# A hybrid decoder layer: sixth product, row loads and ScalarE order moved, first-half gate multiplies from GpSimd to VectorE

## The chip, the cores and the metric

The kernel runs on one core of one Trainium2 chip. The metric is device time in microseconds (us) of one execution, as the median of three. A core has a matrix engine (TensorE, PE in the profile, with its weight loads shown as PEld), three engines for element work (VectorE = DVE, ScalarE = ACT, GpSimd = POOL) and an engine that here only issues DMAs (SyncE = SP). Each engine takes its instructions in the order in which they were written, and waits for the others by semaphores.

## The reference

The layer normalises its input, projects it once, sends the columns through two mixers, gates both and projects back. Cut to what matters:

```python
xn = rms_norm(x, ln_g)                                    # x: 2048 x 1024
b, c, xc, gc, xl, gl = split(xn @ w_in)                   # w_in: 1024 x 6144
y_conv = b * causal_conv3(c * xc)
y_conv = headwise_rms_norm(y_conv, 8, conv_out_g) * silu(gc)
u = causal_conv4(xl) + lru_conv_b                         # 16 heads of 64
r, i = sigmoid(u @ w_a + b_a), sigmoid(u @ w_i + b_i)     # block-diagonal
log_a = 8 * r * log_sigmoid(lam)
h = scan(exp(log_a), sqrt(-expm1(2 * log_a)) * (i * u))   # h_t = a_t h_(t-1) + drive_t
y_lru = headwise_rms_norm(h, 16, lru_out_g) * silu(gl)
out = rms_norm(x + concat(y_conv, y_lru) @ w_out, final_g)
```

All of it is float32. The two silus (a sigmoid and a multiply) are the "gates" of the title.

## The kernel before

**Products.** A float32 product is made of three matmuls on rounded pieces: each operand is split into a high and a low part (`th`, `tl` for the moving side T, the two halves of a tile `s` for the stationary side S), and `mm` (L1014) issues high-high, high-low and low-high. One product over four blocks `j` is so 12 matmuls of 128x128 by 128x512. Four output quarters are made of seven such products (numbers 0 to 6) instead of eight by sums and differences of the operands' quarters; `s_plan` makes S's sums, `TPrep`, `bit` and the class `Change` make T's.

**Steps.** The program is 64 steps. Steps 0 to 23 are the first half of the positions: for each of 8 blocks `k` one step `l` (recurrent unit, `lru`), `a` (`conv_a`, c and x of the convolution) and `b` (`conv_b`, b and its gate). Steps 24 to 47 do the same for the second half, steps 48 to 63 (`outp`) the output projection in two phases. Steps 0 to 2 are written out with eight products (`plain`, of eight slots of 12 matmuls, with the side work in `after1` and `after2`). Then a step has slots for products 0, 6 (that of the step before, put off), 1, 3, 2, 4, 5. T is changed at steps 24, 48 and 56: such a step has eight plain products, the next one (called late) six in the order 0, 4, 5, 1, 3, 2, and meanwhile `Change.slot` casts the new T. Its `sixth` subtracts and casts the T of product 6, which the step after the late one (26, 50, 58) uses first.

**Order.** All five engines run in written order (`manual_schedule`). `at(n, f)` puts `f` off by n slots, `tick` runs what is due at a slot's start, and `prep(n, s)` makes piece s of a step's S. `defer(f)` holds `f` back while `held` is a list, and `release` runs it. A product's result lies in a PSUM bank; products 0, 1 and 2 of a step add up in one bank, and ScalarE copies what stands there between them (`q`, `u`, `rr`, L1315 to L1321), so TensorE has to wait with the next product of that bank until the copy is done. `put` takes a finished quarter to the mixer. There, `silu` multiplies gate and sigmoid (`gl<-gl,sg`, `gb<-gb,sg`), on GpSimd except in step 24; `gates` issues four small matmuls into two banks of their own, which `sigs` frees with four sigmoids (`r`, `i`, L758); and `m1` (L832) and `mj` (L835) are the width-3 convolution. In `outp`, `load` brings the rows `xr` (the residual) that are added to the result `ob`.

**Bits.** The T pieces of products 1 and 2 for the first half are 16 small jobs (`bits`: subtractions `traw<-traw`, casts `th` at L1160, low parts `tl`), done two to a slot by `do_bits` from the first slot of step 1 on.

## Time and profile before

| | us |
|---|---|
| three runs | 1316.51, 1317.4, 1314.1 |
| median | 1316.51 |
| the profiled execution | 1314.92 |
| its span, first to last instruction | 1313.1 |
| busy: TensorE | 1289.5 (98%) |
| busy: VectorE | 1046.0 (80%) |
| busy: ScalarE | 748.7 (57%) |
| busy: GpSimd | 250.0 (19%) |

The profile is of one execution. Its span is 1.8 us shorter than that execution's own time, and that time is 1.6 us under the median. Rows of the timeline show the start in us from the span's start, the duration in us, engine, line, operation, output and inputs, shapes, and in brackets the idle time of the engine before it with what ended the idle time. `SPq` rows are DMA issues. Rows of the windows view show for each engine its busy us and how many of its instructions fall in the stretch, then the granted TensorE clock (1.00 is full speed), the DMA engines' share and GB/s.

### The profile page before, as it was taken

What the parts mean: (1) busy time and instruction counts of PE and PEld (TensorE: products, weight loads), DVE (VectorE), ACT (ScalarE), POOL (GpSimd) and SP (SyncE); (2) the same over time, 40 slices, a digit from 0 to 9 for tenths busy, and PEclk for the clock granted to TensorE, in tenths of its full rate; (3) what the DMA queues carried; (4) which work ended last, traced back from release to release, by engine and by line L of the source; (5) the groups of instructions that cost most, each with busy time, mean ns of one, the idle gap of its engine ahead of it and who ended that gap; (6) DMA issues with size and microseconds to landing.
All of it is one profiled execution on the core that took longest, in us unless ns stands there. A gap on an engine that the chain in (4) does not pass through costs nothing.

```text
span 1313.1 us, 16711 instructions
## 1 busy us (share of the span) xinstructions
PE 1289.5 (98%) x5688; PEld 1061.0 (81%) x5688; DVE 1046.0 (80%) x1284; ACT 748.7 (57%) x1141; POOL 250.0 (19%) x189
## 2 busy tenths in 40 slices
PE   7989999999999999999999999999999999999997
PEld 6867888888888888778888888888888888887886
DVE  6789898999999998967666666667559767649886
ACT  7576767576675667566454645454466433445443
POOL 3204243344435441001010110101011000000000
PEclk9989999999999999999999999999999999999999
DMA  7128887898989887651899999999789986697654
GB/s 294 32 90 290 290 286 264 302 350 283 345 302 329 295 301 280 207 199 33 277 318 296 340 352 333 324 355 362 236 271 339 260 261 229 249 402 273 235 179 160
DMA packets 157958, 355.29 MB, mean 271 GB/s; under 512 B 16944, under 2 KB 51760, under 8 KB 157872
## 3 DMA queue, kind: packets, MB, share of 16 engines
q1 hardware_dynamic: 153264, 338.17, 74.4%
q0 software_dynamic: 4320, 15.73, 3.1%
q8 instruction: 45, 0.74, 0.2%
q14 instruction: 41, 0.34, 0.1%
q10 hardware_dynamic: 288, 0.32, 0.1%
HBM read 217.11 MB, written 137.04 MB: 270 GB/s over the span
## 4 chain that ended last, share of the span: by engine, by line
PE 82%; DVE 8%; DMA 5%; ACT 3%; issue 2%; SPq 0%; POOL 0%; ACTq 0%; DVEq 0%
PE bank L1014 79%; DMA s<-so 2%; DVE tl L163 2%; PE gate L751 2%; DVE traw L163 1%; DMA tl<-td 1%; DMA zr<-rsd 1%; DMA xr<-od 1%; DMA fg<-in_final_g_dram 1%; DVE u L723 1%; ACT i L758 0%; DVE s L163 0%; ACT r L758 0%; ACT th L451 0%; PE tp L554 0%
## 5 line engine op out<-in xcount | busy, mean ns | idle before, releaser
L1014 PE MATMUL bank<-th,s 128*128 128x512 f32 x3632 | 1129.6, 390 | 5.7 <-ACT rr L1318 1.6
L1014 PEld LDWEIGHTS bank<-th,s 128*128 128x128 f32 x3632 | 682.7, 188 | 151.7 <-ACT rr L1318 2.5
L1014 PE MATMUL bank<-tl,s 128*128 128x512 f32 x1816 | 708.2, 390 | 1.8 <-DVE tl L163 1.6
L1014 PEld LDWEIGHTS bank<-tl,s 128*128 128x128 f32 x1816 | 341.4, 188 | 74.5 <-DVE tl L163 3.0
L163 POOL TENSOR_TENSOR s<-raw,s 128x512 fp32r<-128x512 f32 x62 | 115.1, 1870 | 231.1 <-ACT s L213 176.0
L213 ACT CAST s<-raw 128x512 fp32r<-128x512 f32 x140 | 85.4, 618 | 48.4 <-PE bank L1014 32.8
L163 POOL TENSOR_TENSOR gb<-gb,sg 128x1024 f32<-128x1024 f32 x16 | 43.4, 2712 | 335.5 <-ACT sg L682 335.5
L163 DVE TENSOR_TENSOR s<-raw,s 128x512 fp32r<-128x512 f32 (+1 forms) x125 | 91.6, 755 | 10.6 <-ACT s L1073 6.7
L163 DVE TENSOR_TENSOR s<-s,s 128x512 fp32r<-128x512 f32 x105 | 86.6, 824 | 2.1 <-ACT s L213 1.5
L163 DVE TENSOR_TENSOR tl<-traw,th 128x512 fp32r<-128x512 f32 x85 | 60.8, 748 | 19.4 <-ACT th L451 13.4
L213 ACT CAST s<-s 128x512 fp32r<-128x512 f32 x105 | 64.7, 616 | 4.3 <-DVE s L163 4.0
L723 DVE SCALAR_TENSOR_TENSOR u<-xl,pt,u 128x1024 f32<-128x1024 f32 x48 | 61.3, 1278 | 6.1 <-ACT u L719 5.5
L835 DVE SCALAR_TENSOR_TENSOR t<-p,pt,t 128x1024 f32<-128x1024 f32 x32 | 46.5, 1454 | 16.6 <-ACT t L832 15.8
L1315 ACT COPY q<-bank 128x512 f32<-128x512 f32 x58 | 33.9, 584 | 40.9 <-PE bank L1014 31.5
L163 DVE TENSOR_TENSOR st<-u,st 64x512 fp32r<-64x512 f32 x64 | 53.8, 841 | 2.0
L758 ACT ACTIVATE r<-gate,pt 64x512 f32<-64x512 f32 x64 | 43.7, 683 | 17.3 <-PE gate L751 16.5
L1318 ACT COPY rr<-bank 128x512 f32<-128x512 f32 x31 | 18.1, 584 | 53.6 <-PE bank L1014 53.3
L1318 ACT COPY u<-bank 128x512 f32<-128x512 f32 x27 | 15.8, 585 | 52.4 <-PE bank L1014 52.4
L163 DVE TENSOR_TENSOR traw<-traw 128x512 f32<-128x512 f32 x60 | 41.8, 701 | 4.7 <-DMA traw<-in_w_out_dram 3.6
L451 ACT CAST th<-traw 128x512 fp32r<-128x512 f32 x64 | 36.1, 618 | 16.1 <-DVE traw L163 14.2
L758 ACT ACTIVATE i<-gate,pt 64x512 f32<-64x512 f32 x64 | 43.8, 684 | 1.1
L1321 ACT COPY u<-bank 128x512 f32<-128x512 f32 x31 | 18.1, 585 | 43.6 <-PE bank L1014 43.5
(169 smaller groups left out, 1294.1 us busy)
## 6 DMA issues: line engine op xcount, KB each, us to landing
sd<-s SPq DMA_DIRECT2D x151, 512.0 KB
s<-sd SPq DMA_DIRECT2D x151, 512.0 KB
raw<-in_w_in_dram SPq DMA_DIRECT2D x104, 256.0 KB
raw<-yd SPq DMA_DIRECT2D x64, 256.0 KB
traw<-in_w_out_dram SPq DMA_DIRECT2D x64, 256.0 KB
so<-so SPq DMA_DIRECT2D x22, 512.0 KB
s<-so SPq DMA_DIRECT2D x22, 512.0 KB
yd<-gl SPq DMA_DIRECT2D x32, 256.0 KB
```

Source lines behind the costliest of these rows:

```text
L163: (eng or nc.vector).tensor_tensor(out=out, in0=a, in1=b, op=op)
L213: nc.scalar.copy(dst[i][0], val(i))
L451: nc.scalar.copy(self.dst[i, j][0], self.r[i, j])
L723: nc.vector.scalar_tensor_tensor(out=v["u"], in0=o1[:, 1 + j:1 + j + N2], scalar=lw[j], in1=v["u"], op0=ALU.mult, op1=ALU.add)
L751: nc.tensor.matmul(ps[j], v["gw"][n][:, j, :], v["st"][j][:, sl], start=(n == 0), stop=(n == 1))
L758: nc.scalar.activation(out=g_[hi, sl], in_=v["ps"][j][src], func=AF.Sigmoid, bias=pt[src, bias + k:bias + k + 1])
L835: nc.vector.scalar_tensor_tensor(out=tcur["t"], in0=p[:, 2 + j:2 + j + N2], scalar=cw[j], in1=tcur["t"], op0=ALU.mult, op1=ALU.add)
L1014: nc.tensor.matmul(bank, a[:, js], b, start=start and n == 0, stop=stop and n == 2, skip_group_check=more)
L1315: nc.scalar.copy(q1, bk["A"])
L1318: nc.scalar.copy(u2, bk["A"])
L1321: nc.scalar.copy(rr, bk["A"])
```

## The change

The change moves instructions and removes none but for the engine of 16 multiplies. In its parts:

1. First half (`h == 0`): the 16 multiplies of gates and sigmoids in `lru` and `conv_b`, each 128x1024, go from GpSimd to VectorE.
2. Bits: two to a slot in the first six slots of step 1 and then one to a slot in step 2, instead of two to a slot in all of step 1.
3. `hi(5)`, the cast of a step's S piece 5, is deferred behind the ScalarE copy `q`; in late steps of the output, casts of T and S go behind `rr` and `u`.
4. Step 26: product order 0, 3, 6, 1, 2, 4, 5. `sixth` subtracts all four blocks in the late step and casts all four one slot later. `m1` is deferred behind the copy `u`.
5. Step 56: `load` two to three slots sooner (ticks 2 and 3, not 5 and 6).

```diff
@@ s_plan
-                lambda: hi(5),
+                lambda: defer(lambda: hi(5)),
@@ class Change
-        def sixth(self, *js):
-            for j in js:
+        def sixth(self):
+            for j in range(NB):
                 tt(self.r[6, j], self.r[6, j], self.r[1, j], ALU.subtract)
-            self.cut([(6, j) for j in js])
+            at(1, lambda: self.cut([(6, j) for j in range(NB)]))
...
             if q == 21:
-                self.sixth(0, 1)
-                at(1, lambda: self.sixth(2, 3))
+                self.sixth()
@@ lru, put
-                silu(g, late, nc.vector if h and late else None)
+                silu(g, late, nc.vector if late or not h else None)
@@ conv_a, put
-                at(1, m1)
+                at(1, lambda: defer(m1))
@@ conv_b, put
-                silu(g)
+                silu(g, 0, None if h else nc.vector)
@@ outp
-            at(5, lambda: load(0))
-            at(6, lambda: load(1))
+            sooner = 3 if ph == 1 and m == 2 else 0
+            at(5 - sooner, lambda: load(0))
+            at(6 - sooner, lambda: load(1))
@@ after1
-            do_bits(2)
+            if s < 6:
+                do_bits(2)
@@ after2
-            do_bits(2)
+            do_bits(1)
@@ main loop
+            if kind != "o" and n > 1 and opens(n - 2):
+                slots = (0, 3, 6, 1, 2, 4, 5)
...
+                if i == 1 and slots[2] == 6:
+                    held[0] = []
                 tick()
...
                 if late:
-                    change.slot(16 + s)
+                    if i != 1 or kind != "o":
+                        change.slot(16 + s)
...
                 elif s == 0:
+                    held[0] = []
                     prep(n, 6)
...
                 elif s > 0:
-                    held[0] = [] if i == 2 else None
-                    prep(n + 1, s - 1)
+                    if i == 2 and not late:
+                        held[0] = []
+                    if i != 2 or kind != "o" or not late:
+                        prep(n + 1, s - 1)
...
-                if s == 1 and not late:
+                if i == 6 and not late and s < 3:
...
                 if i == 0:
                     q1 = sm_q1[0] = sm("q1")
                     nc.scalar.copy(q1, bk["A"])
+                    release()
                 elif i == 1:
                     u2 = sm_u2[0] = sm(("u2", "rr")[n % 2])
                     nc.scalar.copy(u2, bk["A"])
+                    release()
+                    if late and kind == "o":
+                        change.slot(16 + s)
...
                     if late:
                         put(12, bk["D"], rr)
+                        if kind == "o":
+                            prep(n + 1, s - 1)
```

How the order moves is seen at three places. The first is ScalarE in step 1 and at the start of step 2, from the copy of the bank that holds quarter 22 to the convolution `t<-p`. `th<-traw` is a bit's cast, `r` and `i` are the sigmoids that free the gate banks. Before:

```order
L814 COPY xx<-bank 128x512
L814 COPY p<-bank 128x512
L1160 CAST th<-traw 128x512
L1073 CAST s<-raw 128x512
L1160 CAST th<-traw 128x512
L814 COPY xx<-bank 128x512
L758 ACTIVATE r<-gate,pt 64x512
L758 ACTIVATE i<-gate,pt 64x512
```

and with the change:

```order
L813 COPY xx<-bank 128x512
L813 COPY p<-bank 128x512
L1073 CAST s<-raw 128x512
L813 COPY xx<-bank 128x512
L757 ACTIVATE r<-gate,pt 64x512
L757 ACTIVATE i<-gate,pt 64x512
```

The two casts of bits now stand behind these sigmoids, one after `t<-p`, one after the second set of sigmoids.

The second place is ScalarE in steps 25 and 26 (the change of T between the halves), first from the cast of the recurrent unit's `u` on. Before:

```order
L734 CAST st<-u 64x1024 x2
L451 CAST th<-traw 128x512 x2
L1321 COPY u_5065<-bank 128x512
L451 CAST th<-traw 128x512 x2
L1315 COPY q_5099<-bank 128x512
```

and with the change:

```order
L733 CAST st<-u 64x1024 x2
L1334 COPY u_5059<-bank 128x512
L451 CAST th<-traw 128x512 x4
L1324 COPY q_5099<-bank 128x512
L757 ACTIVATE r<-gate,pt 64x512
```

The bank's copy `u` has moved ahead of the casts for the sixth product. A few rows on, from the last sigmoid of the first set, there stood before:

```order
L758 ACTIVATE i<-gate,pt 64x512
L620 CAST rt<-sums 128x512
L832 ACTIVATE t<-p,pt 128x1024
L1318 COPY u_5149<-bank 128x512
L758 ACTIVATE r<-gate,pt 64x512
L758 ACTIVATE i<-gate,pt 64x512
```

and with the change:

```order
L757 ACTIVATE i<-gate,pt 64x512
L619 CAST rt<-sums 128x512
L757 ACTIVATE r<-gate,pt 64x512
L757 ACTIVATE i<-gate,pt 64x512
L757 ACTIVATE r<-gate,pt 64x512
L757 ACTIVATE i<-gate,pt 64x512
L1328 COPY u_5180<-bank 128x512
L831 ACTIVATE t<-p,pt 128x1024
```

The convolution `t<-p` has moved behind the second set of sigmoids and behind the next copy.

The third place is SyncE's issues in step 56, `xr` being the residual rows, `tl<-td` T's pieces, `s<-so` S's pieces, `raw` and `zr` the inputs of a later step's S. Before:

```order
L518 DMA tl<-td_133 128x512
L239 DMA s<-so_125 128x1024
L894 DMA xr<-od_138 128x1024
L239 DMA s<-so_125 128x1024
L307 DMA raw<-yd_86 128x512 x2
L297 DMA zr<-rsd_89 128x1024
L307 DMA raw<-yd_86 128x512 x2
L297 DMA zr<-rsd_89 128x1024
L894 DMA xr<-od_139 128x1024
```

and with the change:

```order
L239 DMA s<-so_125 128x1024
L893 DMA xr<-od_138 128x1024
L517 DMA tl<-td_130 128x512
L517 DMA tl<-td_131 128x512
L517 DMA tl<-td_132 128x512
L517 DMA tl<-td_133 128x512
L893 DMA xr<-od_139 128x1024
L239 DMA s<-so_125 128x1024 x2
L307 DMA raw<-yd_86 128x512 x2
```

The first row load has moved ahead of four T pieces and one S piece, the second ahead of two S pieces, four `raw` and two `zr`.

## The prediction

> **What bounds the kernel.** I read the page first: busy times, then the chain that ended last.

> ```profile
> PE 1289.5 (98%) x5688; PEld 1061.0 (81%) x5688; DVE 1046.0 (80%) x1284; ACT 748.7 (57%) x1141; POOL 250.0 (19%) x189
> ...
> PE 82%; DVE 8%; DMA 5%; ACT 3%; issue 2%; SPq 0%; POOL 0%; ACTq 0%; DVEq 0%
> ```

> TensorE works in 98% of the span and carries 82% of the chain. The change takes no matmul away, so it can only win what TensorE loses in waits or at a lower clock: 1313.1 - 1289.5 = 23.6 us of idle time, part of it at the start and the end, where nothing is changed. The second view is that of the waits, for TensorE alone (us in total, times, longest):

> ```profile
> PE gate L751 <- ACT i L758: 3.6, 2, 3.4
> ...
> PE bank L1014 <- ACT rr L1318: 1.6, 2, 1.3
> ...
> PE bank L1014 <- DVE xx L163: 1.3, 1, 1.3
> PE bank L1014 <- DVE ob L163: 1.1, 1, 1.1
> PE norm_ps L627 <- ACT i L758: 0.8, 1, 0.8
> ```

> These are few and short. Only seven waits matter, and each lies at a place that the change touches. The third view is TensorE's timeline there. For the longest wait, with two rows of the windows view behind it:

> ```profile
> 69.61 0.40 PE L1014 MATMUL bank<-tl,s 128*128 128x512 f32 x1
> ...
> 73.25 0.39 PE L1014 MATMUL bank<-th,s 128*128 128x512 f32 x1
> 77.05 0.79 PE L751 MATMUL gate<-st,bh 128*128 128x512 f32 x1 [3.41 <-ACT i L758]
> ...
> 84.46 0.39 PE L1014 MATMUL bank<-tl,s 128*128 128x512 f32 x1
> ```

> ```profile
> 76.00:80.00 4.00, 2.77 (x6) 1.76 (x7) 1.99 (x4) 3.92 (x7) 0.00 (x0) 0.62 0.02 4
> 80.00:84.00 4.00, 4.00 (x12) 3.09 (x11) 3.93 (x5) 3.81 (x7) 0.10 (x1) 0.53 0.00 0
> ```

> From 69.61 to 73.25 sixteen matmuls start, so one takes (73.25 - 69.61) / 16 = 0.2275 us at full clock. From 73.25 to 84.46 only 18 start (one, 4 of the gates, 13 of products) in 11.21 us, where 18 x 0.2275 = 4.1 would do. **The place costs 7.1 us**, twice what the list of waits says: 77.05 - 73.25 - 0.23 = 3.57 is the wait, and 3.55 is the clock after it, 0.62 and 0.53 of full speed in the two windows.

> **Place A, steps 1 and 2 (6.6 us).** The gate matmul waits for sigmoids that free its bank. ScalarE's queue ahead of them:

> ```profile
> 73.17 0.62 ACT L1160 CAST th<-traw 128x512 fp32r<-128x512 f32 x1 [2.02 <-DVE traw L163]
> ...
> 74.62 0.62 ACT L1160 CAST th<-traw 128x512 fp32r<-128x512 f32 x1 [0.31 <-DVE traw L163]
> 75.15 0.58 ACT L814 COPY xx<-bank 128x512 f32<-128x512 f32 x1
> 75.62 0.68 ACT L758 ACTIVATE r<-gate,pt 64x512 f32<-64x512 f32 x1
> ```

> Two casts of bits stand there, both idle until VectorE has made their input. The change puts both behind the sigmoids: 2.02 + 0.31 of waiting and 2 x 0.53 of casting go, and the first sigmoid starts at 75.62 - 3.4 = 72.2. VectorE is ahead of this point by another 0.6, worked out below. First sigmoid then at 71.6, first bank free two sigmoids (1.4) later at 73.0, second at 74.4. TensorE is there at 73.25 + 0.23 = 73.5 and needs the second bank at 73.9. It loses about 0.5 instead of 7.1. The casts, moved, come due where products 1 and 2 of step 3 need them, seven slots of 12 x 0.2275 us later at least.

> The trace shows that a 3.4 us wait is followed by a slower clock; the wait of 1.32 quoted for place B is not (granted clock 1.00 over that stretch). Between the two nothing is measured. If 2 us of waiting were left, the place would still cost 2.0 with the clock kept and 2.0 + 3.55 = 5.6 with it lost: gains of 5.1 or 1.5. I keep 1.5 to 7.1 as the ends and take 6.6. [...]

> **VectorE instead of GpSimd (0 us by itself).** Rows for what a multiply costs and what it frees:

> ```profile
> 57.89 2.41 POOL L163 TENSOR_TENSOR gl<-gl,sg 128x1024 f32<-128x1024 f32 x1 [2.89 <-ACT sg L682]
> ...
> 403.38 2.88 POOL L163 TENSOR_TENSOR gb<-gb,sg 128x1024 f32<-128x1024 f32 x1 [3.05 <-ACT sg L682]
> ```

> ```profile
> 58.35 2.50 DVE L163 TENSOR_TENSOR s<-raw,s 128x512 fp32r<-128x512 f32 x1 [2.27 <-ACT s L1073]
> ...
> 403.92 2.89 DVE L163 TENSOR_TENSOR raw<-raw 128x512 f32<-128x512 f32 x1
> ...
> 551.02 1.22 DVE L163 TENSOR_TENSOR gl<-gl,sg 128x1024 f32<-128x1024 f32 x1
> ```

> ```profile
> 318.00:377.00 59.00, 59.00 (x262) 48.77 (x261) 57.05 (x59) 38.92 (x56) 24.64 (x15) 1.00 0.92 316
> ```

> In step 25 VectorE makes this multiply already: 1.22 us. The first half moves 16 of them, 19.5 us in all. But a VectorE subtraction that meets GpSimd's multiply ends only with it: 2.50 and 2.89 us, against 0.68 for the same shape elsewhere (the copy-add `xx` of place B). Each multiply that leaves GpSimd so frees 1.8 to 2.2 us, about 2 x 16 = 32. VectorE's net is -12 us at that rate, +19.5 if nothing came back; both ends are kept, and I take the first, as two different multiplies show it. Over a whole period of three steps (318 to 377) TensorE is busy 59.00 of 59.00 and VectorE 57.05, so a freer VectorE gains TensorE nothing there. At place A it is what gives the 0.6: 58.35's 2.50 becomes 0.68 and 1.22 is added ahead of the `st` pieces.

> **`hi(5)` behind `q` (0 us).** ScalarE has the cast ready a slot later; product 5 comes five slots after it, which is the cover.

> **Place B, steps 25 and 26 (3.1 us).**

> ```profile
> 550.35:569.97 19.62, 17.06 (x73) 12.97 (x72) 13.22 (x18) 10.88 (x17) 0.00 (x0) 1.00 0.56 193
> ```

> ```profile
> 555.48 0.50 PE L1014 MATMUL bank<-th,s 128*128 128x512 f32 x1 [1.32 <-DVE xx L163]
> ...
> 566.70 0.71 PE L627 MATMUL norm_ps<-rt,sel 128*96 128x256 f32 x4 [0.82 <-ACT i L758]
> ```

> ```profile
> 552.88 1.23 ACT L451 CAST th<-traw 128x512 fp32r<-128x512 f32 x2 [4.37 <-DVE traw L163]
> ```

> ```profile
> 554.74 0.68 DVE L163 TENSOR_TENSOR xx<-bank,u 128x512 f32<-128x512 f32 x1
> 555.34 0.68 DVE L163 TENSOR_TENSOR p<-bank,u 128x512 f32<-128x512 f32 x1
> ```

> Five slots (60 matmuls), 8 of the gates and 4 of half width stand in these 19.62 us; 70 x 0.2275 = 15.9, so 3.7 are lost, more than the idle 1.32 and 0.82, since the sixth product's T comes piece by piece and restarts are slow. With product 3 put ahead, the sixth starts at 550.35 + 24 x 0.2275 + 4 x 0.2275 = 556.7. Its bank is free at 555.34 + 0.68 = 556.0 and its low parts follow at 0.6 us each from 556.6, where a block of three matmuls takes 0.68: hardly a wait. The copy `u` no longer stands behind the casts that idled 4.37. The wait of `norm_ps` goes, as sigmoids come ahead of `t<-p`. New is that product 2 follows product 1 directly, and needs the copy between (0.6 us, with the four `norm_ps` matmuls as cover): 0.3 to 0.6 lost. What `t<-p` delays (two `mj` on VectorE, then product 4's `t`) has a slot to spare. 3.7 - 0.6 = 3.1; ends 1.0 (T still 1.3 late, the copy uncovered) and 3.4.

> **Place C, steps 56 to 58 (2.7 us), and step 49 (0.3 us).**

> ```profile
> 1180.49:1194.37 13.88, 11.53 (x49) 8.85 (x48) 13.77 (x23) 6.38 (x12) 1.06 (x2) 1.00 0.89 336
> ```

> ```profile
> 1184.68 0.50 PE L1014 MATMUL bank<-th,s 128*128 128x512 f32 x1 [1.30 <-ACT rr L1318]
> 1191.51 0.50 PE L1014 MATMUL bank<-th,s 128*128 128x512 f32 x1 [1.05 <-DVE ob L163]
> ```

> ```profile
> 1168.93 1.23 DVE L163 TENSOR_TENSOR ob<-ob,xr 128x1024 f32<-128x1024 f32 x1 [4.79 <-DMA xr<-od]
> ...
> 1177.08 1.22 DVE L163 TENSOR_TENSOR ob<-ob,xr 128x1024 f32<-128x1024 f32 x1 [2.93 <-DMA xr<-od]
> ...
> 1190.77 1.28 DVE L163 TENSOR_TENSOR ob<-bank,u 128x512 f32<-128x512 f32 x2
> ```

> ```profile
> 1183.52 0.62 ACT L213 CAST s<-s 128x512 fp32r<-128x512 f32 x1 [1.11 <-DVE s L163]
> ```

> ```profile
> 1161.09 0.32 SPq L894 DMA_DIRECT2D xr<-od  x1
> ...
> 1168.90 0.32 SPq L894 DMA_DIRECT2D xr<-od  x1
> ```

> 48 matmuls in 13.88 us lose 13.88 - 10.92 = 3.0. VectorE idles 4.79 and 2.93 for row loads that take about 8 us from issue (1161.09 to 1168.93; 1168.90 to 1177.08). Issued some 6 and 9 us sooner they land before they are wanted. What is late next are `raw` and `zr`, now behind the second load: 0.5 MB at the 336 GB/s of the window is 1.6 us. So of the 7.7 us VectorE gets back some 2. That is enough: `rr`, behind the cast at 1183.52, was some 1.4 late, and `ob<-bank` at 1190.77, moved ahead of two subtractions besides (1.2), was some 1.2 late. The two S loads that the second row load passes are issued several slots ahead of their products. I take 2.7 of 3.0, ends 1.0 and 3.0. In step 49 the smaller `rr` wait (1.6 - 1.3 = 0.3) goes by the reordering.

> **The sum.** 6.6 + 3.1 + 2.7 + 0.3 = 12.7. The profiled execution took 1314.92 (span 1313.1), so 1302.2; the median of the runs is 1.6 higher, so **1303.8**. With the high ends, 7.1 + 3.4 + 3.0 + 0.3 = 13.8: 1302.7; with the low ones, 1.5 + 1.0 + 1.0 = 3.5: 1313.0.

> **The rivals.** *The sigmoids stay late.* If something else holds the sigmoids (the `st` pieces, the copy `xx`), 2 us of wait remain and the gain at A is 5.1 or 1.5: 1305.3 to 1308.9. For it: five instructions of two engines stand close there. Against: the idle times in the rows lie on the casts.

> *VectorE is late in step 3.* TensorE reaches step 3 some 6.6 us sooner, VectorE has the same list, fully packed from 80 us on (3.93 of 4.00 in the second window). If T's and S's last pieces come that much later than wanted, A is given back: 12.7 - 6.6 = 6.1, 1310.4, and with half of B lost too, 1312.0. For it: that list. Against: VectorE idles 2.0 us (1.99 of 4.00 in the first window) just for the late `t`, and 1.8 more came back before.

> *VectorE becomes the bound, slower.* A period has 59.00 - 57.05 = 1.95 us to spare and gets 2 x 1.22 = 2.44. If nothing comes back, and a multiply on VectorE now itself waits about one us for GpSimd's remaining subtractions, a period lacks 2 x 2.2 - 1.95 = 2.5 us, 17 over seven periods; A and B are then lost in VectorE's queue, and C's 3.0 remains: 1316.5 + 17 - 3 = 1330. It decides once a multiply costs 1 us more than it frees (1.95 / 2). The rows say that it frees 0.6 to 1.0 more than it costs.

> **How the numbers follow.** The forecast gets 0.60, late sigmoids 0.20, VectorE late in step 3 0.15, VectorE as bound 0.05. A measurement here tells a change from none at about 0.3%, 4 us. Forecast and late sigmoids are faster by more, and of the third case 0.06; its other 0.09 (with B or C short too) is within. Faster 0.86, same 0.09, slower 0.05. The range goes from 1300 (all high ends, and the 2.4 us by which the fastest run lies under the median) to 1311.

> **What would show it.** A: no wait over 1 us ahead of the gates near 73, and clock 1.00 from 5 to the end; else that step fails. Period: VectorE's busy share no higher than 57 of 59, no subtraction of 2.9 us under `gb`. B: the five slots from step 26's start in about 16.5 us. C: `ob<-ob,xr` with no wait for `xr`, no `rr` wait. New waits of TensorE between 90 and 140 us, or in the periods to 500, would make the prediction wrong.

## The result and the profile after

| | before | after |
|---|---|---|
| median of four runs, us | 1315.91 (1314.1 to 1317.4) | 1302.21 (1301.72 to 1303.73) |
| profiled execution, us | 1314.92 | 1301.72 |
| its span, us | 1313.1 | 1299.7 |

The changed kernel takes 0.9898 of the time before, with a 95% interval of 0.9883 to 0.9912. The medians differ by 13.7 us, the spans by 13.4. Forecast were 12.7 us and 1303.8.

The page of the changed kernel, busy times and chain:

```profile
PE 1283.7 (99%) x5688; PEld 1059.5 (82%) x5688; DVE 1032.8 (79%) x1300; ACT 747.6 (58%) x1141; POOL 208.0 (16%) x173
...
PE 94%; DMA 3%; DVE 1%; ACT 1%; issue 0%; POOL 0%; SPq 0%; ACTq 0%
```

TensorE carries 94% of the chain (82% before). VectorE has 16 instructions more and is busy 13.2 us less. Now TensorE's waits:

```profile
PE tp L553 <- DVE x L536: 3.3, 3, 2.2
...
PE bank L1014 <- ACT q L1324: 0.7, 1, 0.7
...
PE bank L1014 <- ACT rr L1328: 0.3, 1, 0.3
PE bank L1014 <- ACT u L1328: 0.2, 1, 0.2
```

The first is the start of the program, which nothing touched; over the runs of this document it is 1.8 to 3.3 us. Of the seven waits that the prediction listed, the ones at `gate`, `xx`, `ob` and `norm_ps` are gone, and the two at `rr` have shrunk to one of 0.3.

**Place A.** TensorE at the second gates and in step 3, then the windows over the place:

```profile
72.88 0.39 PE L750 MATMUL gate<-st,bh 128*128 128x512 f32 x1
...
73.42 0.50 PE L750 MATMUL gate<-st,bh 128*128 128x512 f32 x1
...
93.90 0.50 PE L1014 MATMUL bank<-th,s 128*128 128x512 f32 x1 [0.67 <-ACT q L1324]
```

```profile
72.00:76.00 4.00, 4.00 (x18) 3.06 (x17) 2.27 (x4) 3.96 (x7) 0.00 (x0) 1.00 0.02 4
76.00:80.00 4.00, 4.00 (x19) 3.30 (x19) 3.91 (x6) 3.08 (x6) 0.10 (x1) 1.00 0.00 0
```

The gates wait for nothing that the profile marks (3.41 before), the clock stays at 1.00 (0.62 and 0.53 before), and the second product of step 3 starts at 93.90. Before it started here, also behind a short wait for the copy `q`:

```profile
101.47 0.50 PE L1014 MATMUL bank<-th,s 128*128 128x512 f32 x1 [0.73 <-ACT q L1315]
```

That is 7.6 us sooner. What made it so, on ScalarE and VectorE:

```profile
70.10 0.60 ACT L813 COPY xx<-bank 128x512 f32<-128x512 f32 x1
70.58 0.69 ACT L757 ACTIVATE r<-gate,pt 64x512 f32<-64x512 f32 x1
```

```profile
58.30 0.69 DVE L163 TENSOR_TENSOR s<-raw,s 128x512 fp32r<-128x512 f32 x1 [2.19 <-ACT s L1073]
...
61.92 1.22 DVE L163 TENSOR_TENSOR gl<-gl,sg 128x1024 f32<-128x1024 f32 x1
...
64.50 2.12 DVE L163 TENSOR_TENSOR st<-u,st 64x512 fp32r<-64x512 f32 x3
```

The first sigmoid starts at 70.58 (75.62 before), straight behind the copy. The subtraction at 58.30 takes 0.69 (2.50 before), and `st` starts 1.46 sooner (65.96 before).

**Places B and C.** The same five slots from step 26's start, and the same four slots of place C (the last two of step 57 and the first two of step 58), as windows:

```profile
542.57:559.11 16.54, 16.30 (x74) 13.25 (x72) 11.67 (x17) 11.08 (x17) 0.00 (x0) 1.00 0.67 228
1168.65:1180.37 11.72, 11.42 (x49) 8.67 (x47) 11.65 (x20) 6.46 (x12) 1.06 (x2) 1.00 1.02 384
```

B takes 16.54 us (19.62 before), C 11.72 (13.88). In C the waits for the row loads and for the copy `rr` read (this `rr` is the copy behind product 1, whose tile has that name in odd steps):

```profile
1153.82 1.23 DVE L163 TENSOR_TENSOR ob<-ob,xr 128x1024 f32<-128x1024 f32 x1 [1.52 <-DMA xr<-od]
1164.22 1.22 DVE L163 TENSOR_TENSOR ob<-ob,xr 128x1024 f32<-128x1024 f32 x1
```

```profile
1171.82 0.50 PE L1014 MATMUL bank<-th,s 128*128 128x512 f32 x1 [0.30 <-ACT rr L1328]
```

Step 49's shorter wait for `rr` is gone too, 0.6 us with the restart (before, the second matmul behind the wait starts 1.05 us after the last one ahead of it, 1027.30 to 1028.35, where two starts take 0.46 elsewhere). 7.6 + 3.1 + 2.2 + 0.6 = 13.5, against the 13.4 by which the span fell. That they agree so well is partly chance. Counted by the product matmuls, of which both kernels have the same number, the last one starts 13.8 us sooner (1305.67 before, 1291.84 after): 0.5 more are gained at smaller places, near 194 and 868 us above all, 0.2 are lost right behind the four slots, and the stretch from the last product matmul to the end takes 0.4 longer.

### The profile page after: what moved, and what is told of

It is laid out like the page before. It is cut to its first block, busy times and chain, and to the rows that moved or that the text cites. A ratio compares the mean times of both kernels' runs of the same rounds, so it can differ in the third digit from the quotient of the medians.

```text
span 1299.7 us, 16676 instructions
## 1 busy us (share of the span) xinstructions
PE 1283.7 (99%) x5688; PEld 1059.5 (82%) x5688; DVE 1032.8 (79%) x1300; ACT 747.6 (58%) x1141; POOL 208.0 (16%) x173
## 4 chain that ended last, share of the span: by engine, by line
PE 94%; DMA 3%; DVE 1%; ACT 1%; issue 0%; POOL 0%; SPq 0%; ACTq 0%
PE bank L1014 91%; PE gate L750 2%; DMA s<-so 1%; DMA tl<-td 1%; DMA xr<-od 1%; DMA zr<-rsd 0%; PE tp L553 0%; DVE ob L163 0%; ACT junk L531 0%; DMA x<-in_x_dram 0%; DVE s L163 0%; DVE raw L163 0%; DVE ob L976 0%; ACT traw L558 0%; DVE ob L936 0%
## 5 line engine op out<-in xcount | busy, mean ns | idle before, releaser
L1014 PE MATMUL bank<-th,s 128*128 128x512 f32 x3632 | 1127.0, 390 | 2.0 <-ACT q L1324 0.7
L1014 PEld LDWEIGHTS bank<-th,s 128*128 128x128 f32 x3632 | 681.9, 188 | 146.1 <-ACT q L1324 1.4
L1014 PE MATMUL bank<-tl,s 128*128 128x512 f32 x1816 | 707.4, 390 | 1.6 <-DVE tl L163 1.4
L1014 PEld LDWEIGHTS bank<-tl,s 128*128 128x128 f32 x1816 | 340.9, 188 | 73.7 <-DVE tl L163 2.4
L163 POOL TENSOR_TENSOR s<-raw,s 128x512 fp32r<-128x512 f32 x62 | 116.5, 1890 | 281.0 <-ACT s L213 251.8
L213 ACT CAST s<-raw 128x512 fp32r<-128x512 f32 x140 | 84.6, 618 | 35.6 <-PE bank L1014 21.1
L163 DVE TENSOR_TENSOR s<-raw,s 128x512 fp32r<-128x512 f32 (+1 forms) x125 | 85.1, 703 | 10.3 <-ACT s L1073 6.6
L163 DVE TENSOR_TENSOR s<-s,s 128x512 fp32r<-128x512 f32 x105 | 74.9, 713 | 1.9 <-ACT s L213 1.9
L163 DVE TENSOR_TENSOR tl<-traw,th 128x512 fp32r<-128x512 f32 x85 | 58.3, 719 | 19.8 <-ACT th L451 10.4
L213 ACT CAST s<-s 128x512 fp32r<-128x512 f32 x105 | 65.0, 619 | 7.4 <-DVE s L163 7.4
L163 POOL TENSOR_TENSOR gb<-gb,sg 128x1024 f32<-128x1024 f32 x8 | 20.0, 2503 | 298.4 <-ACT sg L681 260.6
L163 DVE TENSOR_TENSOR st<-u,st 64x512 fp32r<-64x512 f32 x64 | 52.4, 819 | 2.0
L163 DVE TENSOR_TENSOR raw<-raw,zr 128x512 f32<-128x512 f32 x64 | 41.1, 682 | 6.4 <-DMA zr<-rsd 6.4
L163 DVE TENSOR_TENSOR traw<-traw 128x512 f32<-128x512 f32 x60 | 41.7, 699 | 3.1 <-DMA traw<-in_w_out_dram 2.1
```

What stands on the lines that cost most here:

```text
L163: (eng or nc.vector).tensor_tensor(out=out, in0=a, in1=b, op=op)
L213: nc.scalar.copy(dst[i][0], val(i))
L1014: nc.tensor.matmul(bank, a[:, js], b, start=start and n == 0, stop=stop and n == 2, skip_group_check=more)
```

## The experiments

Each time is compared with runs of the kernel before on the same chip, whose medians were 1314.95 to 1315.26.

### The multiplies alone

The kernel before, with only the engine of 16 multiplies changed:

```diff
-                silu(g, late, nc.vector if h and late else None)
+                silu(g, late, nc.vector if late or not h else None)
...
-                silu(g)
+                silu(g, 0, None if h else nc.vector)
```

> The kernel before with one part of the change alone: the first half's 16 multiplies on VectorE. Theory (the multiplies gain nothing by themselves; at place A they bring VectorE, and with it the sigmoids, 0.6 to 1.5 us ahead): the gates of step 2 still wait 2.1 to 3.0 us instead of 3.57. If the clock is lost after that wait as well, 1 us faster than before (ratio 0.999); if it is kept, 4 to 5 us faster (0.9965). VectorE's stretched subtractions under gb and gl are gone and its first-half busy time falls by about 10 us. Rival 1 (the multiplies carry the whole gain): 10 us faster or more, 0.992. Rival 2 (VectorE becomes the bound): slower than before, waits of TensorE for VectorE in every period of three steps.

Measured: 1313.11, ratio 0.9983 (0.9973 to 0.9992), 1.9 us faster. The wait ahead of the gates fell from 3.41 to 2.55, as VectorE made the casts' input sooner. The clock still halved; the two windows are aligned to where it did:

```profile
76.63 0.50 PE L751 MATMUL gate<-st,bh 128*128 128x512 f32 x1 [2.55 <-ACT i L758]
```

```profile
73.99:77.40 3.41, 0.83 (x3) 0.30 (x2) 3.18 (x6) 3.15 (x6) 0.00 (x0) 1.00 0.00 0
77.40:80.81 3.41, 2.78 (x7) 2.20 (x8) 1.59 (x2) 3.37 (x6) 0.00 (x0) 0.50 0.03 5
```

So the multiplies are worth something by themselves, but do not save the clock. Where the gain lies needs care, as this execution also ran at half speed from 15.96 to 19.37 us, ahead of place A, and the kernel before did not. From the last product matmul ahead of step 2's first gates (67.30 here, 66.31 before) to step 3's second product (101.47 in both) it is 1.0 us faster, which is the gain forecast for a lost clock. Another 0.8 lies at place B, which the forecast did not name: TensorE's wait for `xx` in step 26 is 0.52 (1.32 before), and it is about 0.5 in all four profiles with the multiplies on VectorE and step 26 in its old order.

### The spread bits alone

```diff
-            do_bits(2)
+            if s < 6:
+                do_bits(2)
...
-            do_bits(2)
+            do_bits(1)
```

> The kernel before with the bits' spread alone (two to a slot in six slots of step 1, then one to a slot). Theory (the two casts hold the sigmoids): first sigmoid near 72.2 us, TensorE loses about 1.2 us at the gates instead of 7.1, clock stays at 1.00: 5 to 6 us faster than before, ratio 0.9955 to 0.996. Rival (VectorE's lateness holds the sigmoids): a wait of 2 us or more is left, and at most 2 us are gained if the clock is lost.

Measured: 1310.93, ratio 0.9964 (0.9951 to 0.9977), 4.0 us (5 to 6 forecast). The gates wait 0.67 once, the clock stays at 1.00, and step 3's second product starts at 95.21, 6.3 us sooner than before. Then over 1 us is given back in step 3, at a wait that neither kernel has and that the forecast did not see:

```profile
107.37 0.50 PE L1014 MATMUL bank<-th,s 128*128 128x512 f32 x1 [0.98 <-ACT u L1322]
```

### The change without the multiplies

The changed kernel with the multiplies back on GpSimd:

```diff
-                silu(g, late, nc.vector if late or not h else None)
+                silu(g, late, nc.vector if h and late else None)
...
-                silu(g, 0, None if h else nc.vector)
+                silu(g)
```

> The changed kernel with the first half's 16 multiplies back on GpSimd. Theory: VectorE's busy time is 10 us higher, and TensorE loses 0.7 to 1.0 us at place A (second gate bank) and up to 0.5 at place B: 1 to 1.5 us slower than the changed kernel, ratio to before 0.990 to 0.991. Rival (VectorE's relief carries the gain): 5 us slower than the changed kernel or more, ratio over 0.994.

Measured: 1303.90, ratio 0.9912 (0.9898 to 0.9927); its profiled span is 1301.5, 1.8 us over the changed kernel's. The intervals of the two ratios overlap, so the times alone do not show the difference; the rows do. Step 3's second product starts at 95.22, 1.3 us later than in the changed kernel. The gates wait 0.67, and the wait in step 3 is there again, 1.20 us. Its rows, GpSimd, VectorE and ScalarE in turn, with TensorE last:

```profile
100.71 3.38 POOL L163 TENSOR_TENSOR gb<-gb,sg 128x1024 f32<-128x1024 f32 x1
```

```profile
101.75 2.89 DVE L163 TENSOR_TENSOR s<-raw 128x512 f32<-128x512 f32 x1
```

```profile
105.40 0.62 ACT L213 CAST s<-s 128x512 fp32r<-128x512 f32 x1 [2.48 <-DVE s L163]
...
106.98 0.56 ACT L1334 COPY u<-bank 128x512 f32<-128x512 f32 x1
```

```profile
107.60 0.50 PE L1014 MATMUL bank<-th,s 128*128 128x512 f32 x1 [1.20 <-ACT u L1334]
```

The subtraction under GpSimd's multiply takes 2.89 us, the cast that needs what VectorE makes next idles 2.48, the copy `u` stands behind the cast, and TensorE behind the copy. With the restart this costs 1.5 us (106.01 to 107.93 for two starts, 1.92 instead of 0.46), so 1.3 + 1.5 = 2.8 are lost by 117 us. That the span differs by 1.8 alone comes from place C, where this execution did better by 0.9 with the same instructions (see place C under the prediction). The windows view over the same 4 us, first of this kernel, then of the changed one:

```profile
101.00:105.00 4.00, 4.00 (x19) 3.31 (x18) 3.97 (x3) 1.06 (x1) 3.09 (x1) 1.00 0.50 133
```

```profile
101.00:105.00 4.00, 4.00 (x19) 3.30 (x19) 3.96 (x7) 3.73 (x7) 0.00 (x0) 1.00 0.87 239
```

VectorE is equally busy in both, 3.97 and 3.96 us, but three instructions fall in the stretch in the one and seven in the other. Busy time alone does not tell an engine that works from one that is held up.

### Multiplies and bits together

The two diffs above in the kernel before, nothing else:

> The kernel before with two parts of the change together: the 16 multiplies on VectorE and the bits two to a slot in six slots and then one to a slot. Alone, the multiplies gained 1.9 us and the spread bits 4.0 us, the latter with a new wait of 0.98 at 106.0 in step 3. My theory: together they are the whole of place A, 7.5 us, because the wait at 106 is made by the multiplies of GpSimd: ratio 0.9943, no wait at 106, granted clock 1.00 from 5 us to the end, TensorE starting step 3's second product near 93.9 to 94.2. Rival (the two parts only add up, and the rest of the 7.6 comes from another part of the change): 5.9 us, ratio 0.9955, with a wait over 0.5 us left in steps 2 or 3.

Measured: 1307.20, ratio 0.9942 (0.9929 to 0.9956), 8.1 us. The ratio does not exclude the rival's 0.9955, which lies inside the interval; the trace does. TensorE does not wait in step 2, nor at 106 in step 3. One wait is left between 60 and 120 us:

```profile
94.03 0.50 PE L1014 MATMUL bank<-th,s 128*128 128x512 f32 x1 [0.87 <-ACT q L1316]
```

The row lies 7.4 us sooner than before. By the medians the two parts alone gave 1.9 + 4.0 = 5.9 and 2.2 come only when both are there, but the ratios, times 1315 us, give 2.2 + 4.7 = 6.9 of 7.6, so the times leave the size open. By the product matmuls from 59 to 117 us the parts gain 1.0 and 4.7 alone and 7.4 together, so 1.7 come only together: with the bits spread, TensorE reaches step 3 so early that VectorE is the late one, and with the multiplies off GpSimd it no longer is. The changed kernel's other 0.1 at this row goes with a shorter wait for `q` (0.67).

### A shorter wait, twice

The multiplies, and the bits two to a slot in seven slots, so that one cast stays ahead of the sigmoids:

```diff
-            do_bits(2)
+            if s < 7:
+                do_bits(2)
...
-            do_bits(2)
+            do_bits(1)
```

> The kernel before with the multiplies on VectorE and the bits two to a slot in seven slots of step 1 instead of six, so that one of the two casts stays ahead of the sigmoids. Theory: a wait of 0.8 to 2 us at the gates, between the 1.3 us that leaves the clock alone and the 3.4 us that halves it. If the clock is kept, 5 to 6 us faster than before (0.996); if it is lost, about 2 (0.9985).

> A second look at the kernel with multiplies on VectorE and bits two to a slot in seven slots, whose waits ahead of the gates near 74 us (1.62 and 0.67 us) left the clock at 1.00 in its first profile, while its times spread over 1308.7 to 1313.9. My theory: whether such a wait halves the clock depends on where a 3.41 us grid of the clock's control falls in this execution. So waits and order of work will be the same, but times spread by some 3.4 us or more again, and this profile may show a granted clock of 0.5 for 3.41 us from about 77 to 83. Rival (the wait's length alone decides): the clock is 1.00 again, and the times lie within 1 us of each other.

Measured: first 1311.43 with runs from 1308.69 to 1313.9, ratio 0.9971 (0.9962 to 0.998); the second time 1310.59, runs from 1309.18 to 1311.38, ratio 0.9959 (0.9943 to 0.9975). In the first ten runs the three slowest (1312.81 to 1313.9) are the three with the lowest mean clock, 0.994 and 0.995; the others have 0.997 to 0.999. The second time the runs spread over 2.2 us, less than the 3.4 forecast and more than the rival's 1. The waits in the two profiles are alike. The first:

```profile
74.31 0.50 PE L751 MATMUL gate<-st,bh 128*128 128x512 f32 x1 [1.62 <-ACT i L758]
...
75.71 0.50 PE L751 MATMUL gate<-st,bh 128*128 128x512 f32 x1 [0.67 <-ACT i L758]
```

```profile
70.54:73.96 3.42, 2.15 (x10) 1.45 (x8) 2.90 (x6) 2.60 (x5) 0.00 (x0) 1.00 0.00 0
73.96:77.37 3.41, 2.39 (x9) 1.70 (x10) 1.56 (x3) 3.35 (x7) 0.00 (x0) 1.00 0.02 5
```

and the second:

```profile
74.52 0.50 PE L751 MATMUL gate<-st,bh 128*128 128x512 f32 x1 [1.61 <-ACT i L758]
...
75.92 0.70 PE L751 MATMUL gate<-st,bh 128*128 128x512 f32 x1 [0.67 <-ACT i L758]
```

```profile
72.64:76.05 3.41, 1.14 (x5) 0.43 (x4) 2.50 (x4) 3.33 (x7) 0.00 (x0) 1.00 0.00 0
76.05:79.47 3.42, 3.42 (x9) 2.65 (x10) 2.36 (x2) 3.38 (x7) 0.00 (x0) 0.50 0.02 5
79.47:82.88 3.41, 3.41 (x17) 2.80 (x16) 3.38 (x7) 2.58 (x5) 0.10 (x1) 1.00 0.00 0
```

One program, the same two waits, and once the clock stays and once it halves for 3.42 us (1.7 lost). From the last product matmul ahead of these gates to step 3's second product, the first profile takes 4.3 us less than the kernel before (72.30 to 96.22, against 73.25 to 101.47), the second 2.7 (72.53 to 98.04). So in these two profiles the length of the wait alone does not decide. How the stretches were chosen is told under the hardware.

### The wait filled with work

The kernel before, with 24 dummy matmuls (128x128, results unused) ahead of the gates that wait. They take no wait away; they keep TensorE busy during it, for 2.78 us as measured (73.08 to 75.86):

```diff
+            if h == 0 and k == 0 and i == 1:
+                spin(24)
```

> The kernel before with 24 idle transposes of 128x128 (about 0.13 us each, 3.1 us) on TensorE just ahead of the second gates of step 2; nothing else is changed, and their result is not used. It fills the 3.57 us wait with work and leaves what is waited for as late as it was. Theory (the wait costs itself and, after it, 3.5 us of halved clock): clock 1.00 at 76 to 84 us, and 3 to 3.5 us faster than before, ratio 0.9975. Rival (the slower clock is not caused by the idling): no faster, 1.000.

Measured: 1313.18, ratio 0.9984 (0.9973 to 0.9995), 1.8 us (3 to 3.5 forecast). The clock stays at 1.00 though ScalarE and VectorE are as late as before; the gates now start at 76.70, 0.84 us after the last dummy:

```profile
72.00:76.00 4.00, 3.86 (x30) 3.38 (x28) 3.93 (x8) 2.86 (x6) 0.00 (x0) 1.00 0.00 0
76.00:80.00 4.00, 2.63 (x10) 1.91 (x11) 1.98 (x4) 3.94 (x7) 0.00 (x0) 1.00 0.01 4
```

In this profile step 3's second product starts 2.9 us sooner (98.61), of which 0.4 lie ahead of the place (the last product matmul ahead of the gates starts at 72.85 and 73.25). So 2.5 us are the clock's share of place A with the wait left in, where the prediction has 3.55: at full clock TensorE has to wait 0.67 for the second gate bank, and at half clock it waited 0.18, so part of what the slow clock took would have been waiting.

### Step 26 alone

The kernel before with the order 0, 3, 6, 1, 2, 4, 5 in step 26, the joined `sixth` and the deferred `m1` (with the lines around `held` and `release` that these need, left out here):

```diff
-            self.cut([(6, j) for j in js])
+            at(1, lambda: self.cut([(6, j) for j in range(NB)]))
...
-                at(1, m1)
+                at(1, lambda: defer(m1))
...
+            if kind != "o" and n > 1 and opens(n - 2):
+                slots = (0, 3, 6, 1, 2, 4, 5)
```

> The kernel before with the parts for steps 25 and 26 alone (product order 0, 3, 6, 1, 2, 4, 5, the joined sixth, the deferred convolution). Theory: the five slots from step 26's start take 16.5 to 17.3 us instead of 19.6 and nothing else changes: 2.3 to 3.1 us faster, ratio 0.9976 to 0.9982. Rival (it needs VectorE's relief at the change of T): gain under 1.5 us, with T's sixth low parts awaited in slot three.

Measured: 1311.84, ratio 0.9976 (0.9965 to 0.9986), 3.1 us. The five slots:

```profile
549.82:566.34 16.52, 16.28 (x73) 13.24 (x72) 12.25 (x18) 11.08 (x17) 0.00 (x0) 1.00 0.64 223
```

Place B is this edit, whole: without the other parts it takes the five slots from 19.62 to 16.52. (The joined `sixth` also acts at the two other changes of T; no gain is seen there.)

### The row loads alone, the output's order alone

```diff
-            at(5, lambda: load(0))
-            at(6, lambda: load(1))
+            sooner = 3 if ph == 1 and m == 2 else 0
+            at(5 - sooner, lambda: load(0))
+            at(6 - sooner, lambda: load(1))
```

> The kernel before with the sooner row loads of step 56 alone. Theory: no wait of VectorE for xr in steps 56 and 57, and the 13.9 us of the four slots near 1180 fall by 1 to 2 us, ratio 0.9985 to 0.9992. Rival (the DMA engines are full there, so what is brought sooner delays what comes next by as much): no gain, 1.000.

Measured: 1314.66, ratio 0.9994 (0.9983 to 1.0005). In the profile VectorE no longer waits for a row load, the wait for `rr` in step 57 is gone, and the one for `ob` is still there:

```profile
1189.54 0.50 PE L1015 MATMUL bank<-th,s 128*128 128x512 f32 x1 [1.04 <-DVE ob L163]
```

The other edit puts the casts of T and S behind `rr` and `u` in the late steps of the output:

```diff
-                    change.slot(16 + s)
+                    if i != 1 or kind != "o":
+                        change.slot(16 + s)
...
-                    prep(n + 1, s - 1)
+                    if i != 2 or kind != "o" or not late:
+                        prep(n + 1, s - 1)
...
+                    if late and kind == "o":
+                        change.slot(16 + s)
...
+                        if kind == "o":
+                            prep(n + 1, s - 1)
```

> The kernel before with the late output steps' order alone (casts of T behind the copy u, casts and low parts of S behind the combine). Theory: the wait for ob at step 58 goes (1.2 us) and that for rr stays, since it hangs on VectorE; step 49 gains 0.3 to 0.5: 1.5 us in all, ratio 0.9989. Rival (the reordering carries all of place C): 2.5 us or more.

Measured: 1314.15, ratio 0.9991 (0.998 to 1.0003). Here `ob` is gone and `rr` stays:

```profile
1185.01 0.50 PE L1014 MATMUL bank<-th,s 128*128 128x512 f32 x1 [1.46 <-ACT rr L1320]
```

Neither can be told from no change by its time. By the profiles, over the same five slots (16.60 us before), the loads give 1.3 and the order 0.8; both together, in the changed kernel, give 2.0. Each edit takes one of C's two waits. The order also takes step 49's wait, 0.6.

### `hi(5)` alone

```diff
-                lambda: hi(5),
+                lambda: defer(lambda: hi(5)),
```

with the `held` and `release` that it needs around the copy `q`.

> The kernel before with only the cast hi(5) put behind the copy q. My theory: 0 us, since ScalarE has slots to spare for this cast: ratio 1.000 (0.9990 to 1.0010), the same seven waits of TensorE in the profile. Rival (q comes sooner in each step and TensorE stops losing some 0.03 us in each of 56 steps): 1.5 us, ratio 0.9989; then the waits and small gaps at the first slots shrink.

Measured: 1315.37, ratio 1.0002 (0.9993 to 1.0011). It is worth nothing here. The profile shows the seven waits, with `rr` at 2.9 us in total (1.6 before), in steps that this edit does not reach. In the other profiles whose kernel leaves place C alone this sum is 1.1 to 2.6, so it varies from run to run.

## Why the prediction was right

| step of the prediction | forecast, us | profile after against before |
|---|---|---|
| place A, steps 1 and 2 | 6.6 | 7.6 |
| VectorE instead of GpSimd, by itself | 0 (and 0.6 inside A) | 2.8 against the run without: 1.3 of A's 7.6, and 1.5 of waiting in step 3 |
| `hi(5)` | 0 | 0 |
| place B | 3.1 | 3.1 |
| place C | 2.7 | 2.2 |
| step 49 | 0.3 | 0.6 |
| sum | 12.7 | 13.5 |

The total came closer than its parts. A and step 49 were 1.3 short, C was 0.5 over, and one step, the multiplies, was valued wrongly in a way that the sum does not show: without them A's gain would not have arrived whole.

**Place A** went by its mechanism: two casts away from the sigmoids, no wait, no slow clock. It was undersized by 1.0, and the failing term is how far VectorE comes ahead, "another 0.6". Only the first subtraction's 1.81 was counted as freed. The two instructions behind it shrank too, 0.88 to 0.69 and 1.22 to 0.69, which gives 2.53 - 1.22 = 1.3, and the rows show 1.46. (The two lay beside GpSimd's small `bh` and `bl`, which stood behind the multiply, at 60.26 and 61.19, and now run before.) So the first sigmoid started at 70.58 and not 71.6, and most of the half microsecond left as a loss was not lost. Another 0.5 lay at step 2's first gates, which the prediction did not look at: from 66.31, the last product matmul ahead of them, to 67.99, the first one behind, the kernel before took 1.68 us, and the changed one takes 1.16 (66.25 to 67.41). No single gap there was long enough for the list of waits. The bits alone leave this loss (1.67 us there), and the multiplies alone take it away (1.16).

One term was over: of the place's 7.1 us the prediction gave 3.55 to the slow clock. The run with the wait filled shows 2.5 there. In the gain at A this does no harm, as wait and clock go together, but it does where a wait is left.

**The 2 us wait.** The prediction left open whether a shorter wait keeps the clock. The runs answer: 2.55 us did not keep it, and 1.62 + 0.67 us kept it in one profile and lost it in another. The place then still cost 7.1 - 4.3 = 2.8 us with the clock kept and 7.1 - 2.7 = 4.4 with it lost, where the prediction had 2.0 and 5.6. The change never came to that point.

**VectorE instead of GpSimd** was the step with a wrong size. The bookkeeping came out: 16 multiplies cost 9.7 us for `gb` and 10.8 for eight `gl` on VectorE, and its busy time fell by 13.2 (forecast 12). The groups that gave most back, before and after:

```profile
L163 DVE TENSOR_TENSOR s<-s,s 128x512 fp32r<-128x512 f32 x105 | 86.6, 824 | 2.1 <-ACT s L213 1.5 <-PE bank L1014 0.6
...
L163 DVE TENSOR_TENSOR raw<-raw 128x512 f32<-128x512 f32 x41 | 42.7, 1042 | 0.2
```

```profile
L163 DVE TENSOR_TENSOR s<-s,s 128x512 fp32r<-128x512 f32 x105 | 74.9, 713 | 1.9 <-ACT s L213 1.9
...
L163 DVE TENSOR_TENSOR raw<-raw 128x512 f32<-128x512 f32 x41 | 31.7, 773 | 0.2
```

But "a freer VectorE gains TensorE nothing" was read from one period at 318 us and carried over to the steps where A's gain arrives. Step 3 is not such a period: without the multiplies TensorE waits 1.20 there. The rival *VectorE is late in step 3* had seen this place. It happens in the kernel with A's bits and without the multiplies, and costs 1.5 us with its restart and not 6.6. The rival *VectorE becomes the bound* needed a multiply to cost more than it frees, which it did not. The row that the prediction asked for, 59 us of a period 7.6 us earlier:

```profile
310.40:369.40 59.00, 59.00 (x261) 48.79 (x260) 55.19 (x62) 38.72 (x56) 19.39 (x13) 1.00 0.91 315
```

VectorE's share fell from 57.05 to 55.19, and no `raw<-raw` ran under a GpSimd `gb` in the first half any more. In this period TensorE has indeed no gain: it is busy 59.00 of 59.00 in both.

**Place B** came out to the tenth: 16.5 us forecast, 16.54 measured. **Place C** was a little short. One sign that the prediction named fails: the first row load still keeps VectorE waiting, 1.52 us (4.79 before), and `rr` still costs TensorE 0.30. This is no limit of the change. In the run without the multiplies, whose instructions at place C are those of the changed kernel, VectorE waits for no row load, TensorE for no `rr`, and the four slots take 10.88 us, which is all that their 48 matmuls need:

```profile
1171.62:1182.50 10.88, 10.88 (x50) 8.87 (x48) 10.81 (x19) 5.90 (x11) 1.06 (x2) 1.00 1.04 404
```

So the gain at C varies from execution to execution, 2.2 in one and 3.0 in the other, around the forecast's 2.7. Why the first row load lands later in the one is open. In step 49 the restart behind the wait was left out: 0.6 and not 0.3.

## What to carry to other kernels

A wait of TensorE can cost well over its length through the clock (here 2.5 us on top of 3.6), so look at the granted clock behind waits like these (here 1.61 us with 0.67 close behind it lost the clock in one profile, 1.32 did not), and take windows of a few microseconds, not the page's forty slices. When a step is made to come sooner, read the queues at the place where it will arrive: what has slack at the old time may be late at the new one. And when two engines work side by side, count instructions per stretch beside busy time, as a held-up instruction counts as busy (here 3.97 us with three instructions, 3.96 with seven).

## What the runs showed of the hardware

**A mostly idle stretch was enough.** TensorE was busy for 1.14, 0.83 and, in the kernel before (73.53 to 76.94), 0.11 us of the 3.41 ahead of a halving. With 2.15, 2.39 and 2.19 us (the last in the kernel with the dummy matmuls, 76.15 to 79.56) the clock stayed. The row loads alone, which leave place A as it was, have a closer pair, full speed behind the first of these stretches and half behind the second:

```profile
72.08:75.50 3.42, 1.49 (x7) 0.91 (x5) 3.35 (x6) 2.08 (x4) 0.00 (x0) 1.00 0.00 0
75.50:78.91 3.41, 1.25 (x4) 0.78 (x5) 2.03 (x4) 3.33 (x6) 0.00 (x0) 1.00 0.00 0
```

But busy time, as the profile has it, does not settle it. With the multiplies alone the clock also halved at 15.96, near the start of the program, behind a stretch with 2.00 us, part of it transposes:

```profile
12.54:15.96 3.42, 2.00 (x9) 0.97 (x7) 3.11 (x5) 2.52 (x5) 1.75 (x1) 1.00 1.01 402
```

What decides it is not shown. The grid fits what the two profiles of the shorter wait do: in the one that kept the clock an edge, 73.96, lies inside the longer wait (72.69 to 74.31), in the other both waits lie between the edges 72.64 and 76.05. That this makes the difference is the author's reading; no run tests it by itself. It would fit part of the scatter of the kernel before as well. Of the kernels that leave place A as it was, one profile (the row loads alone) has 3.41 us at half speed there, the others 6.8 to 6.9 by their windows (6.83 in the kernel before). And of 31 runs of the kernel before on one chip, the ten with a mean clock of 0.994 or 0.995 took 1316.8 us on average, the four with 0.998 took 1313.3.

Idle gaps of 1.61 and 0.67 us close together were enough for a halving (those ahead of 74.52 and 75.92 in the second profile of the shorter wait).

**Subtractions of VectorE that started under GpSimd's multiply ended 0.55 us after it.** The rows give 57.89 + 2.41 = 60.30 against 58.35 + 2.50 = 60.85, then 406.26 against 406.81, and in the changed kernel with the multiplies back on GpSimd 104.09 against 104.64. In the changed kernel the first of them, with no multiply beside it, takes 0.69 (at 58.30). So in these rows it is over when the multiply is, give or take its own length, as if it did next to nothing until then. Not every instruction is held up: at 129.69 in the kernel before, `xx<-bank,rr`, with one input in a PSUM bank, took 0.69 inside a multiply that ran from 128.60 to 131.45, and `raw<-raw` at 605.39, with no such input, took 0.69 inside one that ran from 604.99 to 608.33. What makes the difference no run here shows.
